# An encoder block with 64 streamed experts: the upper half of four late expert matrices loaded in transfers of eight partitions

## The chip, the core and the metric

The kernel runs on one core of a Trainium2 chip. The core has five engines that run their own instruction streams: TensorE (PE, matrix products; PEld is its weight load), VectorE (DVE), ScalarE (ACT), GpSimd (POOL) and SyncE (SP), which here does little but issue transfers. Sixteen DMA engines move the data between the chip's memory and the on-chip buffer, which has 128 partitions. The metric is the device time of one execution in microseconds, lower is better. Before the change it is 1477.58 us, the median of three runs (1474.58 to 1478.69).

## The reference, cut to what matters

One layer on 512 tokens of width 1024, in float32: a normalised projection, a convolution branch and an attention branch that are gated, merged and projected, and then a mixture of experts. There are 64 experts in 8 groups; every token takes the best group and in it the two best experts. Each expert has three matrices of 1024 x 512, 1024 x 512 and 512 x 1024, 2 MB each.

```
def mixer_block(u, ...):
    cb, cc, cx, q, k, v, gc, ga = split_columns(u @ w_in)
    y_conv = (cb * depthwise_conv_centred(cc * cx, conv_w)) @ w_conv_out
    y_attn = bidirectional_gqa(rope(rmsnorm(q)), rope(rmsnorm(k)), v) @ w_attn_out
    return (sigmoid(gc) * y_conv + sigmoid(ga) * y_attn) @ w_o

def hier_moe(u, w_group, w_router, w1, w3, w2):
    g = argmax(u @ w_group)                      # a group for each token
    top_v, top_i = top_k((u @ w_router)[g], 2)   # two experts in it
    def expert_block(xb, e):
        return (silu(xb @ w1[e]) * (xb @ w3[e])) @ w2[e]
    ...                                          # weighted sum of both experts

h = x + mixer_block(rmsnorm(x), ...)
out = h + hier_moe(rmsnorm(h), ...)
```

## The kernel before

The first 540 us or so are the mixer: projections of all 512 tokens with weights that SP loads in pieces of 512 KB and that ACT and DVE split in two parts. Behind it come the 64 experts, one after the other (the loop `for e in range(NE)`). For an expert, PE gathers up to 32 tokens with a selection matrix (`o_x`), multiplies them with w1 and w3 (`h`, 64 matrix products each; `hidden`), ACT and DVE form the gated product `gt`, and PE multiplies that with w2 (`y`, 32 products; `expert`). After every four experts PE scatters the results back to the tokens (`o_c`), and DVE adds them to `acc`. The last expert is written out apart (`last_expert`): its products are mixed with the scatter of the experts before it, and each finished piece of `acc` is stored at once.

The weights are numbered in the order of their use: matrix `i` belongs to expert `i // 3`, and `i % 3` says which of w1, w3 and w2 it is. `load_weight(i)` issues the load on SP's queue as one transfer of 128 partitions with 16 KB each (`nc.sync.dma_start`, line 601); the last matrix, 191, goes in two halves by columns. Nine buffers take turns, so the load of matrix `i` must wait until PE has read the matrix that was in the buffer. The loop issues the three loads of an expert ahead of that expert's work in the program, but SP runs ahead of PE as far as its waits allow.

A second wait is set by the framework and isn't in the kernel's text: a transfer that SP issues signals its end on one of eight semaphores, DMAHW0 to DMAHW7, which are taken in turn, and it is issued only when the transfer before it on that semaphore has landed. So at most eight of SP's transfers are under way. SP issues in program order, and what stands behind a waiting transfer waits too.

In the profile's rows all of this kernel's expert matrices are called `w`, and their issues stand at line 601.

Of the kernel before, what the change touches and what calls it, by code (L numbers as in the profile page):

```python
# [19 lines left out]
P = 128  # L20
# [11 lines left out]
CAP = 32  # L32
LOADS = (0, 1, 2, 4, 5)
CUTS = (0, 512, 1024)
OVB = 128
C_CB, C_CC, C_CX, C_Q, C_K, C_V, C_GC, C_GA = 0, 1024, 2048, 3072, 4096, 4352, 4608, 5632

# [2 lines left out]
def block_kernel(ctx, tc, x, norm1_g, w_in, conv_w, q_norm_g, k_norm_g, w_conv_out,  # L40
                 w_attn_out, w_o, norm2_g, w_group, w_router, w1, w3, w2, rope, out):
    nc = tc.nc
# [10 lines left out]
    def slot(i, shape, dt, name):  # L53
        return big.tile(shape, dt, tag=f"s{i}", name=name)
# [524 lines left out]
    wtiles = {}  # L579

    def weight_tile(i):
        shape = [P, 4, D] if i % 3 == 2 else [P, NK, FE]
        nm = f"{names[i % 3]}_{i // 3}"
        if i == len(order):
            return pools["mp"].tile(shape, F32, tag="acc", name=nm)
        return slot(order[(i if i < len(order) else i - 1) % len(order)], shape, F32, nm)

    def weight_source(i, e):
        if i % 3 == 2:
            return w2[e].rearrange("(p c) d -> p c d", c=4)  # L590
        return (w1, w3)[i % 3][e].rearrange("(p j) f -> p j f", j=NK)

    def rows(tile):
        return [tile[:, k, :] for k in range(tile.shape[1])]

    def load_weight(i):
        src = weight_source(i, i // 3)
        tile = weight_tile(i)
        cuts = CUTS if i == 3 * NE - 1 else (0, src.shape[2])
        for c0, c1 in zip(cuts, cuts[1:]):  # L600
            nc.sync.dma_start(tile[:, :, c0:c1], src[:, :, c0:c1])
        wtiles[i] = rows(tile)

    def load_unit(i):
        unit(lambda: load_weight(i))
# [23 lines left out]
    while nload < 10:  # L629
        load_weight(nload)  # L630
        nload += 1
# [137 lines left out]
    def overflow_table():  # L769
# [10 lines left out]
        for i in range(4):  # L780
            V.tensor_scalar(cnt[:, 1:2] if i else nblk[:, 0:1], cnt[:, 0:1], float(CAP + OVB * i), None, op0=OP.is_gt)
            if i:
# [10 lines left out]
        V.tensor_tensor(ov_base, io128[:, :NE], tab2[:, NE:2 * NE], op=OP.subtract)  # L793
        V.tensor_scalar(ov_base, ov_base, float(OVB), float(CAP), op0=OP.mult, op1=OP.add)
        ov_tab = mp.tile([1, NE + 1], I32, name="ov_tab")
# [42 lines left out]
    def slots_of(posm, gq):  # L838
        p0 = mp.tile(shp, F32, tag="p0", name="p0")
        es = slice(4 * gq, 4 * gq + 4)  # L840
        for t in range(NT):
            V.tensor_tensor(p0[:, t], posm[:, t, es, None].to_broadcast(shp[:1] + shp[2:]),
                            io32[:, None, :].to_broadcast(shp[:1] + shp[2:]), op=OP.is_equal)
        return p0
# [126 lines left out]
    for e in range(NE):  # L971
        while nload < min(3 * e + 3, 3 * NE):
            load_weight(nload)
            nload += 1
# [6 lines left out]
        elif e % 4 == 3 and e < NE - 1:  # L981
            p0 = slots_of(posm, e // 4 + 1)
# [12 lines left out]
        if e == 0:  # L995
            posm, W = finish_routing()
            p0 = slots_of(posm, 0)
# [42 lines left out]
```

## Time and profile before

| | us |
|---|---|
| median of the runs (lowest to highest) | 1477.58 (1474.58 to 1478.69) |
| profiled execution, its own time | 1474.83 |
| its span on the core | 1473.0 |
| PE busy in the span | 1207.8 (82%) |
| DVE, ACT, POOL busy | 460.5, 345.8, 88.1 |
| data moved | 449.71 MB |

The span runs from the first to the last instruction; 1.8 us lie around it. The page's second section cuts the span into 40 equal slices of 36.8 us. The DMA line in it gives the busy share of the sixteen DMA engines in tenths, the line under it what they moved. The page's fourth section follows the work that ended last backwards and says by which engine or transfer each part of the span was held. A wait of SP's own queue (SPq) is listed with what ended it. A transfer's landing time is counted from its issue, and so includes the time that it stands in line behind earlier transfers.

### The profile page before, as it was taken

Reading aid. Unit: us, or ns where it says so; the run is one execution under the profiler, and the core shown is the slowest. Engines: PE = TensorE matmul, PEld = TensorE weight load, DVE = VectorE, ACT = ScalarE, POOL = GpSimd, SP = SyncE. Lnnn points to the kernel's source line nnn. Section 1 sums busy time; section 2 is a strip of 40 time slices with the busy share of each in tenths; the row PEclk is TensorE's granted clock in tenths of the full one; section 3 lists DMA queues with packets and bytes.
Section 4 is the critical chain, followed back from the end, with each engine's and each line's share of the span. In section 5 each row is a group of like instructions: output and inputs, shape, how many; then the busy total and the mean of one; then the engine's idle time right before and its main releaser. Section 6 shows DMA issues by size and latency. Waiting matters only on the chain.

```text
span 1473.0 us, 33338 instructions
## 1 busy us (share of the span) xinstructions
PE 1207.8 (82%) x15152; PEld 902.4 (61%) x15152; DVE 460.5 (31%) x927; ACT 345.8 (23%) x716; POOL 88.1 (6%) x128
## 2 busy tenths in 40 slices
PE   7999999999999988888677785876867868678656
PEld 6788888888887866655454553544545545455443
DVE  4466666622225243132122120220211212212103
ACT  4344444422233131111111111111111111111101
POOL 2200000000002001000000000000000000000000
PEclk9999999999999999999898998988989979888989
DMA  6222222333354769999999999999999999999993
GB/s 165 59 86 65 66 70 72 93 110 97 101 193 128 322 237 426 423 427 425 426 426 426 425 426 427 425 427 424 426 426 426 426 424 426 427 425 425 427 412 146
DMA packets 109583, 449.71 MB, mean 305 GB/s; under 512 B 12544, under 2 KB 81152, under 8 KB 84992
## 3 DMA queue, kind: packets, MB, share of 16 engines
q1 hardware_dynamic: 108400, 447.55, 75.2%
q8 instruction: 120, 1.97, 0.5%
q10 hardware_dynamic: 1040, 0.00, 0.0%
q14 instruction: 23, 0.19, 0.0%
HBM read 445.44 MB, written 2.10 MB: 304 GB/s over the span
## 4 chain that ended last, share of the span: by engine, by line
PE 60%; DMA 35%; issue 2%; ACT 1%; DVE 1%; POOL 0%; SPq 0%; ACTq 0%; POOLq 0%; DVEq 0%
DMA w<-in_w 34%; PE o_c L74 8%; PE h L74 7%; PE o_g L74 6%; PE o_x L74 6%; PE y L74 5%; PE o_cb L74 3%; PE o_cx L74 3%; PE o_yc L74 3%; PE o_o L74 3%; PE o_q L74 3%; PE o_cc L74 3%; PE o_ya L74 2%; PE s L74 2%; PE o_pv L74 1%
## 5 line engine op out<-in xcount | busy, mean ns | idle before, releaser
L74 PE MATMUL h<-w,X 128*32 128x128 f32 x8192 | 296.7, 300 | 128.1 <-DMA w<-in_w 111.9
L74 PEld LDWEIGHTS h<-w,X 128*32 128x32 f32 x8192 | 258.8, 121 | 174.7 <-issue 81.7
L74 PE MATMUL y<-w,gt 128*32 128x256 f32 (+1 forms) x2080 | 152.1, 430 | 89.0 <-DMA w<-in_w 69.2
L74 PEld LDWEIGHTS y<-w,gt 128*32 128x32 f32 x2080 | 83.3, 121 | 140.0 <-issue 113.1
L890 ACT COPY Y<-y 32x256 f32<-32x256 f32 x252 | 91.4, 363 | 229.7 <-PE y L74 227.3
L158 DVE TENSOR_TENSOR wl<-raw,wh 128x1024 fp32r<-128x1024 f32 x76 | 98.6, 1298 | 140.8 <-ACT wh L157 139.4
L74 PE MATMUL o_x<-xt,pR 128*32 128x256 f32 x2048 | 133.9, 382 | 8.2 <-issue 4.8
L74 PE MATMUL o_c<-Y,S 128*128 128x512 f32 x256 | 121.9, 629 | 12.3 <-ACT Y L890 11.8
L157 ACT CAST wh<-raw 128x1024 fp32r<-128x1024 f32 x76 | 80.6, 1060 | 203.0 <-PE o_g L74 67.1
L831 DVE TENSOR_TENSOR acc<-o_c,acc 128x512 f32<-128x512 f32 x120 | 83.0, 692 | 114.0 <-PE o_c L74 114.0
L717 DVE STREAM_TRANSPOSE X<-xs 128x256 f32<-128x256 f32 x64 | 28.5, 445 | 281.6 <-PE h L74 244.6
L74 PEld LDWEIGHTS o_x<-xt,pR 128*32 128x32 f32 x2048 | 81.4, 110 | 42.0 <-issue 8.5
L872 DVE TENSOR_TENSOR sp<-h,sg 128x128 f32<-128x128 f32 x64 | 23.3, 364 | 264.3 <-ACT sg L868 264.3
L868 ACT ACTIVATE sg<-h 128x128 f32<-128x128 f32 x64 | 17.7, 277 | 374.6 <-PE h L74 374.6
L74 PEld LDWEIGHTS o_c<-Y,S 128*128 128x128 f32 x256 | 49.6, 200 | 78.1 <-issue 48.7
L74 PE MATMUL o_g<-u,wh 128*128 128x512 f32 x256 | 80.5, 395 | 0.0
L854 POOL TENSOR_TENSOR pR<-p,rstd 128x512 f32<-128x512 f32 x15 | 15.6, 1039 | 711.5 <-PE o_x L74 651.6
L74 PEld LDWEIGHTS o_g<-u,wh 128*128 128x128 f32 x256 | 48.1, 188 | 11.2
L74 PE MATMUL o_g<-u,wl 128*128 128x512 f32 x128 | 50.5, 395 | 0.0
L74 PE MATMUL o_q<-u,wh 128*128 128x512 f32 x128 | 40.3, 396 | 0.0
L74 PE MATMUL o_cc<-u,wh 128*128 128x512 f32 x128 | 40.2, 395 | 0.0
L74 PE MATMUL o_cb<-u,wh 128*128 128x512 f32 x128 | 40.1, 395 | 0.0
(221 smaller groups left out, 1418.7 us busy)
## 6 DMA issues: line engine op xcount, KB each, us to landing
w<-in_w SPq DMA_DIRECT2D x191, 2048.0 KB, 39.1
raw<-in_w_in SPq DMA_DIRECT2D x52, 512.0 KB, 3.8
raw<-in_w_conv_out SPq DMA_DIRECT2D x8, 512.0 KB, 4.1
raw<-in_w_attn_out SPq DMA_DIRECT2D x8, 512.0 KB, 4.1
raw<-in_w_o SPq DMA_DIRECT2D x8, 512.0 KB, 5.8
xt<-in_x SPq DMA_DIRECT2D x4, 512.0 KB, 7.0
w<-in_w SPq DMA_DIRECT2D x2, 1024.0 KB, 36.2
out<-acc SPq DMA_DIRECT2D x8, 256.0 KB, 2.1
```

The costliest lines, as they stand in the source:

```text
L74: return TE.matmul(o, l, r, start=start, stop=stop)
L157: A.copy(h, r)
L158: V.tensor_tensor(l, r, h.bitcast(F32), op=OP.subtract)
L717: V.transpose(X.rearrange("p j s -> p (j s)"), xs.rearrange("p j i -> p (j i)"))
L831: V.tensor_tensor(acc_at(t, n), o, xt[:, t, nsl] if first else acc_at(t, n), op=OP.add)
L854: eng.tensor_tensor(pR, p0.rearrange("p t e s -> p t (e s)"), rstd2[:, :, None].to_broadcast([P, NT, P]), op=OP.mult)
L868: A.activation(sg, h[:, 0:P], AF.Silu)
L872: V.tensor_tensor(sp.rearrange("p (c i) -> p c i", c=4), h[:, P:2 * P].rearrange("p (i c) -> p c i", c=4), sg.rearrange("p (i c) -> p c i" ...
L890: A.copy(d, y[32 * q:32 * q + 32, 0:256])
```

## The change

Four matrices, 174, 175, 177 and 178, are no longer loaded in one transfer. They are w1 and w3 of experts 58 and 59. Each is loaded as one transfer of its lower 64 partitions and eight transfers of eight partitions each for the upper 64. Matrix 176 (w2 of expert 58) and all others are loaded as before.

```
@@ -32,6 +32,7 @@
 LOADS = (0, 1, 2, 4, 5)
 CUTS = (0, 512, 1024)
+EIGHTHS = (174, 175, 177, 178)
 OVB = 128
@@ -596,6 +597,12 @@
     def load_weight(i):
         src = weight_source(i, i // 3)
         tile = weight_tile(i)
+        if i in EIGHTHS:
+
+            for p0, p1 in [(0, 64)] + [(b, b + 8) for b in range(64, P, 8)]:
+                nc.sync.dma_start(tile[p0:p1], src[p0:p1])
+            wtiles[i] = rows(tile)
+            return
         cuts = CUTS if i == 3 * NE - 1 else (0, src.shape[2])
```

On SP's queue before the change, this is the place from the second matrix of expert 57 to the first of expert 59. A row names the buffer and, behind the arrow, the source (w1, w3 or w2), the shape, and the semaphores that the issue waits for (DMAHW: the earlier transfer on the same semaphore; PE: the buffer's last reader).

```order
L601 DMA w3_57_11456<-in_w3 128x4096 [waits DMAHW3_49,PE_49]
L601 DMA w2_57_11458<-in_w2 128x4096 [waits DMAHW4_49,PE_49]
L601 DMA w1_58_11574<-in_w1 128x4096 [waits DMAHW5_49,PE_49]
L601 DMA w3_58_11576<-in_w3 128x4096 [waits DMAHW6_49,PE_49]
L601 DMA w2_58_11578<-in_w2 128x4096 [waits DMAHW7_49,PE_49]
L601 DMA w1_59_11694<-in_w1 128x4096 [waits DMAHW0_49,PE_49]
```

Every transfer has its own semaphore here and is a whole matrix, so eight under way are eight matrices.

The same place on SP's queue after the change, from the first matrix of expert 58 to the lower half of the second:

```order
L608 DMA w2_57_11458<-in_w2 128x4096 [waits DMAHW4_49,PE_49]
L603 DMA w1_58_11574<-in_w1 64x4096 [waits DMAHW5_49,PE_49]
L603 DMA w1_58_11574<-in_w1 8x4096 [waits DMAHW6_49]
L603 DMA w1_58_11574<-in_w1 8x4096 [waits DMAHW7_49]
L603 DMA w1_58_11574<-in_w1 8x4096 [waits DMAHW0_49]
L603 DMA w1_58_11574<-in_w1 8x4096 [waits DMAHW1_49]
L603 DMA w1_58_11574<-in_w1 8x4096 [waits DMAHW2_49]
L603 DMA w1_58_11574<-in_w1 8x4096 [waits DMAHW3_49]
L603 DMA w1_58_11574<-in_w1 8x4096 [waits DMAHW4_49]
L603 DMA w1_58_11574<-in_w1 8x4096 [waits DMAHW5_49]
L603 DMA w3_58_11584<-in_w3 64x4096 [waits DMAHW6_49,PE_49]
```

The matrix takes nine semaphores where it took one. The seven issues from DMAHW6 to DMAHW4 wait for the seven whole matrices before it, the last one of which is w2 of expert 57; the eighth one (DMAHW5) waits for the lower half of its own matrix.

## Rows read from the trace of the kernel before

**Rows 1.** The page: the chain that ended last, shares by engine and line.

```profile
PE 60%; DMA 35%; issue 2%; ACT 1%; DVE 1%; POOL 0%; SPq 0%; ACTq 0%; POOLq 0%; DVEq 0%
DMA w<-in_w 34%; PE o_c L74 8%; PE h L74 7%; PE o_g L74 6%; PE o_x L74 6%; PE y L74 5%; PE o_cb L74 3%; PE o_cx L74 3%; PE o_yc L74 3%; PE o_o L74 3%; PE o_q L74 3%; PE o_cc L74 3%; PE o_ya L74 2%; PE s L74 2%; PE o_pv L74 1%
```

**Rows 2.** The same chain in order of time, near the end: start, length, what.

```profile
1366.88 36.93 DMA w<-in_w
...
1403.87 39.57 DMA w<-in_w
1443.44 0.14 issue
1443.58 1.81 PE h L74 x32
...
1461.06 5.36 PE o_c L74 x12
```

**Rows 3.** Stretches of the span: busy time by engine, granted clock, DMA share, GB/s.

```profile
core 0: us, PE busy (x) PEld busy (x) DVE busy (x) ACT busy (x) POOL busy (x), PEclk, DMA share, GB/s
1200.00:1280.00 80.00, 57.36 (x977) 39.43 (x970) 13.65 (x32) 12.16 (x34) 2.51 (x5) 0.84 1.01 426
...
1430.00:1434.00 4.00, 1.13 (x34) 0.83 (x24) 0.00 (x0) 0.00 (x0) 0.00 (x0) 0.94 0.99 390
1434.00:1438.00 4.00, 3.14 (x52) 2.34 (x46) 0.47 (x2) 0.28 (x1) 0.00 (x0) 0.63 0.61 253
1438.00:1442.00 4.00, 1.93 (x32) 1.13 (x32) 0.22 (x1) 1.45 (x4) 0.00 (x0) 1.00 0.50 205
1442.00:1446.00 4.00, 2.42 (x33) 1.89 (x34) 0.00 (x0) 0.00 (x0) 0.00 (x0) 0.72 0.50 213
1446.00:1450.00 4.00, 4.00 (x38) 1.83 (x37) 1.38 (x2) 0.00 (x0) 0.00 (x0) 0.85 0.49 183
1450.00:1454.00 4.00, 4.00 (x41) 1.69 (x39) 2.07 (x3) 0.00 (x0) 0.00 (x0) 1.00 0.28 108
```

**Rows 4.** DMA queues (packets, MB, share of 16 engines' span) and issues (KB, us).

```profile
q1 hardware_dynamic: 108400, 447.55, 75.2%
q8 instruction: 120, 1.97, 0.5%
...
w<-in_w SPq DMA_DIRECT2D x191, 2048.0 KB, 39.1
...
out<-acc SPq DMA_DIRECT2D x8, 256.0 KB, 2.1
...
wr<-in_w_group SPq DMA_DIRECT2D x1, 32.0 KB, 3.0
...
g2j<-in_norm_g SPq DMA_DIRECT2D x1, 4.0 KB, 2.4
```

**Rows 5.** Waits of SP's queue from 1200 us on: total us, times, longest.

```profile
SPq L601 <- DMA w<-in_w: 162.0, 43, 4.9
...
SPq L601 <- PE h L74: 29.4, 11, 5.0
SPq L601 <- PE y L74: 11.2, 4, 3.0
```

**Rows 6.** The tile w: SP's issues, min/median/max ns, and the landing times.

```profile
L601 SPq DMA_DIRECT2D w<-in_w x193: 327/328/6116, 291.0 to 1418.5; - x193
...
DMA to landing us min/median/max: 7.9/39.1/40.8
```

**Rows 7.** PE near the end, in order of time: idle before, and what ended it.

```profile
1389.16 3.59 PE L74 MATMUL h<-w,X 128*32 128x128 f32 x64 [2.85 <-DMA w<-in_w]
```

More of the change, by code (lines that the diff above doesn't have):

```diff
@@ L34 @@
 CUTS = (0, 512, 1024)
+EIGHTHS = (174, 175, 177, 178)
 OVB = 128
@@ L598, in load_weight @@
         tile = weight_tile(i)
+        if i in EIGHTHS:
+            for p0, p1 in [(0, 64)] + [(b, b + 8) for b in range(64, P, 8)]:
+                nc.sync.dma_start(tile[p0:p1], src[p0:p1])
+            wtiles[i] = rows(tile)
+            return
         cuts = CUTS if i == 3 * NE - 1 else (0, src.shape[2])
```

## The prediction

> **What bounds the kernel now.** I read the shares of the chain that ended last first [rows 1]: after PE, the loads of the expert matrices are the largest part of it, 34% of the span. Its end in order of time [rows 2] then shows where: from 1366.88 us to 1443.44 us it is almost nothing but these loads. After the last wait for a load, PE, ACT and DVE need 1473.0 - 1443.44 = 29.6 us to the end, and the change touches nothing there. The stretches [rows 3] show why the loads bind: in the steady part the DMA share is 1.01 and the engines move 426 GB/s, while PE is busy for 57.36 of 80 us. A matrix of 2048.0 KB [rows 4], 2,097,152 bytes, thus takes 4.92 us, one engine brings 426 / 16 = 26.6 GB/s, and PE uses 72% of that time. PE waits before a set of products for the load, not the other way round [rows 7]. So what delays or hastens the last loads moves the end by as much.
>
> Two more things are to be seen. First, SP's issues wait mainly for earlier transfers: 162.0 us against 40.6 us for PE [rows 5]. A matrix lands 39.1 us after its issue [rows 6], which is eight times 4.92 us: eight transfers are under way, and all eight count, whatever their size. Second, the sixteen engines don't end together [rows 3]: the share falls from 0.99 at 1430 to 1434 us to 0.50 from 1438 to 1446 us, at 205 to 213 GB/s, although the last matrix had been issued by 1418.5 us [rows 6]. I read this as eight engines that are done near 1434.5 us and eight that work until about 1452 us: a lag of some 18 us (0.61 over 1434 to 1438 us is a full share for 0.9 us and half of it after; 0.28 from 1450 us on is half for 2.2 us). A cause of that size is there: the instruction queue took 0.5% of 16 engines' span [rows 4], 0.005 x 16 x 1473 = 118 us of engine time, or 14.7 us on each of eight engines. Let me call them the early and the late half.
>
> **The change part by part.** *Issues.* Four transfers become 36, so 32 more issues at 0.327 us [rows 6], 10.5 us of SP in all. Nine for a matrix take 2.9 us, less than the transfer of one; SP has nothing else to do there, so I cost them at nothing. Without that cover it would be up to 10.5 us.
>
> *Bytes.* The same, but they may go to other engines. An eighth is 128 KB in eight rows. I assume eight engines with one row each, all eight times the same ones; if these are the early half, the early half gets 64 KB more and the late half 64 KB less for each engine and matrix: four times 2.46 us either way, 9.84 us.
>
> *The new wait.* The lower half of matrix 174 and the first seven eighths are issued when the eight whole matrices before it land, one every 4.92 us. In these 39.4 us the early half gets only the lower half (2.46 us) and seven eighths. It has 39.1 - 18 = 21 us of older work in line, and then runs dry: its lead is not passed on to the late half but lost as idle time. The eighth one waits for the lower half of 174, which the late half moves 2.46 us after matrix 173, and matrix 175 stands behind it on SP. From issue to first data I take 1.5 us (a store of 256.0 KB lands after 2.1 us [rows 4], of which 0.6 us is the transfer at 426 GB/s). So both halves are empty about 4.0 us after 173 has landed, and only then goes on. From there eight transfers under way are hardly one matrix.
>
> *The price of an eighth.* The trace before has no such transfer. From below: eight engines at 26.6 GB/s each, 0.62 us. From above: in the steady part sixteen engines fill 128 partitions, eight partitions get 26.6 GB/s, and nothing shows that they can take more; then it's 131,072 B / 26.6 GB/s = 4.92 us. In between stands that a group of four neighbouring partitions shares one way in: two engines' rates, 2.46 us. I take 2.46 us. The nearest rows are those of the small transfers, whatever holds them: they landed after 2.1 us for 256 KB, 2.4 us for 4 KB and 3.0 us for 32 KB [rows 4], none sooner.
>
> [...]
>
> *The sum,* from the landing of matrix 173 to that of 191, 18 matrices, 88.6 us before. After: 4.0 us until the flow starts again; 25 eighths (the last of 174, and those of 175, 177, 178) at 2.46 us, 61.5 us; three lower halves at 2.46 us, 7.4 us; 14 whole matrices at 4.92 us, 68.9 us. That is 141.8 us, or +53.2 us. The first seven eighths of 174 hide in the wait, but if ways in are shared, they take their time from the late half, which fills the upper partitions at 213 GB/s: 7 x 131,072 B / 213 GB/s = 4.3 us. The late half's instruction packets no longer count in the last 90 us: 1% of them, -1 us. So +56.5 us: 1474.83 + 56.5 = 1531.3 us for the profiled execution. That one lies 2.75 us under the median of its kernel; the median comes to 1534 us. PE follows: its products for a matrix, at most 3.6 us even at a low clock [rows 7], fit in 4.92 us.
>
> **The rivals.**
>
> *The engines are the limit, not the way in.* An eighth costs 0.62 us, so 25 of them 15.4 us: 4.0 + 15.4 + 7.4 + 68.9 = 95.7 us, +7.1, less 1: +6 us, 1484 us. For it: sixteen engines at 26.6 GB/s is all the rows show, and a limit elsewhere need not exist. Against it: eight engines have never been seen writing to eight partitions. If the late half gets the eighths, nothing of them hides: 4 x 2.46 = 9.8 us, 1487 us. Which half it is no row tells. [...]
>
> *The two halves are evened out* (the other side). The early half ends 9.84 us later, near 1444.3 us, the late one 9.84 us earlier, near 1442.4 us: the loads end 7.9 us before 1452.2 us, and the time is 1470 us. For it: the lag of 18 us is real, and twice 9.84 us is just its size. It decides on the early half having its additional work in line before it runs dry: that needs some 16 transfers under way at 174, and eight are let through. It also needs eighths at 0.62 us.
>
> *All eight partitions share one way in:* 4.92 us an eighth, 25 of them 123 us: 4.0 + 123 + 7.4 + 68.9 = 203.3 us, +114.7 and +3.3 as above, 1596 us. Against it: a way so narrow would have no reserve over the one engine that uses it before.
>
> *The change doesn't do what it says:* an eighth is spread over all sixteen engines. Then no lag is moved, but the waits stay: the same sum with 0.31 us for an eighth, 4.0 + 7.7 + 7.4 + 68.9 = 88.0 us, no change, 1477 us. Eight rows would have to be cut for it.
>
> **How the numbers follow.** Forecast 1534 us, chance 0.58, by itself 1515 to 1560 (the refill of 4.0 us and the sharing of 4.3 us each up to twice, or the eighths partly apart in time). The engine limit, 1481 to 1488 us, 0.23. Evened out, 1470 us, 0.08. One way in, 0.05. No change, 0.03. The rest, 0.03, lies between 1488 and 1515 us. The range from 1480 to 1560 us leaves out the gain, most of no change and the one way, about 0.16. A measurement of this kernel can tell about 0.3%, 4.4 us, from no change. Faster 0.08; same 0.05, with the low edge of the engine limit; slower 0.87.
>
> **What the profile after would show.** SP's waits for `w` at the new line 603, 4.92 us each for the first seven, then about 2.5 us each (0.6 us if the engines are the limit). The landing time of an eighth in the rest near 8 x 2.46 = 20 us. A DMA share near one third to one half, and some 110 GB/s or less, for about 80 us from 1365 us on, then 426 GB/s again. PE waiting some 20 us each for w1 and w3 of expert 58 and 59. The end of the loads without the step at half share, or a shorter one. I would be wrong in kind if the loads ended earlier, and in the price if the stretch at low rate were 25 us long.

## The result and the profile after

The changed kernel takes 1543.86 us, the median of four runs (1528.98 to 1551.09), against 1476.16 us before: a ratio of 1.0437, 95% interval 1.0394 to 1.0480, or +67.7 us. The forecast was 1534 us with a range of 1480 to 1560 us. The profiled execution took 1538.8 us with a span of 1537.0 us, 64.0 us more than before.

First the packets, from the page of the kernel before and then of the changed one.

```profile
DMA packets 109583, 449.71 MB, mean 305 GB/s; under 512 B 12544, under 2 KB 81152, under 8 KB 84992
```

```profile
DMA packets 109839, 449.71 MB, mean 293 GB/s; under 512 B 12800, under 2 KB 81408, under 8 KB 85248
```

The bytes are the same, and there are 256 more packets, all under 512 B. They stand against 32 more transfers, so each adds eight. The two experiments with halves below add four transfers of 64 partitions and 64 packets (12608), 16 for each. I read the small packet as the end of one engine's part in a transfer: an eighth is then the work of eight engines, a half that of sixteen.

Stretches of the changed kernel, with the columns of [rows 3]:

```profile
1340.00:1350.00 10.00, 9.16 (x23) 3.75 (x16) 4.33 (x7) 1.45 (x4) 0.00 (x0) 0.72 1.05 382
1350.00:1360.00 10.00, 7.43 (x182) 5.58 (x184) 2.07 (x5) 1.24 (x3) 0.00 (x0) 1.00 0.80 188
...
1370.00:1380.00 10.00, 7.67 (x182) 5.51 (x178) 1.26 (x4) 0.65 (x2) 0.00 (x0) 1.00 0.47 120
...
1390.00:1400.00 10.00, 0.00 (x0) 0.00 (x0) 0.00 (x0) 0.00 (x0) 0.00 (x0) 0.50 0.97 126
1400.00:1405.00 5.00, 0.00 (x0) 0.00 (x0) 0.00 (x0) 0.00 (x0) 0.00 (x0) 0.50 0.81 157
1405.00:1415.00 10.00, 3.64 (x64) 3.22 (x64) 1.26 (x4) 0.65 (x2) 0.00 (x0) 0.50 0.89 156
1415.00:1425.00 10.00, 3.64 (x32) 1.57 (x32) 0.00 (x0) 1.45 (x4) 0.00 (x0) 0.50 0.63 118
...
1456.00:1490.00 34.00, 19.58 (x356) 13.08 (x356) 4.36 (x12) 4.25 (x14) 0.00 (x0) 0.85 1.01 427
```

Two shorter stretches, inside these:

```profile
1415.30:1419.20 3.90, 3.64 (x32) 1.57 (x32) 0.00 (x0) 0.12 (x1) 0.00 (x0) 0.50 0.49 101
1432.60:1436.20 3.60, 3.55 (x64) 3.22 (x64) 0.00 (x0) 0.00 (x0) 0.00 (x0) 0.50 0.55 114
```

For about 100 us from 1350 us on, the engines move 118 to 188 GB/s where they moved 426; then the old rate is back. The row of 1390 to 1400 us is the one to look at: the DMA share is 0.97 and the rate 126 GB/s. The engines are not out of work, they are held up inside their packets: by the trace's packet records, a packet of 16 KB takes 0.61 us in the steady part, and the 41 that begin between 1395 and 1400 us take 2.1 to 2.2 us each. So the share of 0.97 says here that an engine has a packet open, not that bytes flow at the old rate. Between 1370 and 1380 us, with a share of 0.47, half of them are out of work as well. In the two shorter stretches only about eight engines work (shares of 0.49 and 0.55), on the lower half of matrix 177 and of 178, and they move 101 and 114 GB/s; eight engines alone moved 205 to 213 GB/s in the kernel before [rows 3].

PE in the same place, the first products of matrices 174 to 178, with the wait before each:

```profile
1384.48 1.96 PE L75 MATMUL h<-w,X 128*32 128x128 f32 x64 [2.63 <-DMA w<-in_w]
1405.21 3.64 PE L75 MATMUL h<-w,X 128*32 128x128 f32 x64 [18.77 <-DMA w<-in_w]
1415.38 3.64 PE L75 MATMUL y<-w,gt 128*32 128x256 f32 x32 [6.53 <-DMA w<-in_w]
1432.65 3.64 PE L75 MATMUL h<-w,X 128*32 128x128 f32 x64 [13.63 <-DMA w<-in_w]
1451.53 3.52 PE L75 MATMUL h<-w,X 128*32 128x128 f32 x64 [15.23 <-DMA w<-in_w]
```

Waits of 14 to 19 us stand before w3 of expert 58 and w1 and w3 of expert 59, where [rows 7] had 2.85 us. The products take 3.64 us instead of 1.96 us: the granted clock is 1.00 from 1384 to 1390 us and 0.50 from 1390 to 1450 us, where PE has no product until 1405.21 us. That costs nothing: the next load isn't there.

SP's issues of the eighths (start, length), each row from a short window of its own. An issue that waits for the transfer eight places before it tells when that one landed: the last rise of matrix 169's semaphore is at 1346.67 us, the issue that waits for it at 1346.69 us.

```profile
1341.80 0.27 SPq L603 DMA_DIRECT2D w<-in_w  x1
1346.69 0.27 SPq L603 DMA_DIRECT2D w<-in_w  x1
1354.94 0.27 SPq L603 DMA_DIRECT2D w<-in_w  x1
1363.28 0.27 SPq L603 DMA_DIRECT2D w<-in_w  x1
1369.12 0.27 SPq L603 DMA_DIRECT2D w<-in_w  x1
1375.94 0.27 SPq L603 DMA_DIRECT2D w<-in_w  x1
1379.80 0.27 SPq L603 DMA_DIRECT2D w<-in_w  x1
...
1384.15 0.27 SPq L603 DMA_DIRECT2D w<-in_w  x1
1389.61 0.27 SPq L603 DMA_DIRECT2D w<-in_w  x1
...
1404.99 0.27 SPq L603 DMA_DIRECT2D w<-in_w  x1
1415.26 0.27 SPq L603 DMA_DIRECT2D w<-in_w  x1
1420.51 0.27 SPq L603 DMA_DIRECT2D w<-in_w  x1
...
1432.58 0.27 SPq L603 DMA_DIRECT2D w<-in_w  x1
1437.59 0.27 SPq L603 DMA_DIRECT2D w<-in_w  x1
...
1451.50 0.33 SPq L608 DMA_DIRECT2D w<-in_w  x1
```

The first six rows are the second to the seventh eighth of matrix 174 and mark the landing of the whole matrices 168 to 173. The distance is 4.89 us once, then 8.25, 8.34, 5.84 and 6.82 us: the late engines lose time as soon as the early ones write the parts of 174. The other rows mark, in turn, the landing of

- 174: the lower half (1379.80) and the last eighth (1384.15);
- 175: the lower half (1389.61) and the last eighth (1404.99);
- 176, loaded whole (1415.26);
- 177: the lower half (1420.51) and the last eighth (1432.58);
- 178: the lower half (1437.59) and the last eighth (1451.50).

So a lower half took 5.46, 5.25 and 5.01 us; the eight eighths of a matrix took 15.38, 12.07 and 13.91 us, 1.5 to 1.9 us for one and 1.72 us on average; and the whole matrix 176 took 10.27 us, twice the 4.92 us of the steady part.

### The profile page after: what moved, and what is told of

Read it like the earlier page. It is cut to its first block, busy times and chain, and to the rows that moved or that the text cites. A ratio compares the mean times of both kernels' runs of the same rounds, so it can differ in the third digit from the quotient of the medians.

```text
span 1537.0 us, 33384 instructions
## 1 busy us (share of the span) xinstructions
PE 1224.7 (80%) x15152; PEld 909.6 (59%) x15152; DVE 461.4 (30%) x927; ACT 346.2 (23%) x716; POOL 88.8 (6%) x128
## 4 chain that ended last, share of the span: by engine, by line
PE 52%; DMA 43%; issue 2%; DVE 1%; ACT 1%; another core or an unknown queue 0%; POOL 0%; SPq 0%; ACTq 0%; POOLq 0%; DVEq 0%
DMA w<-in_w 42%; PE h L75 6%; PE o_g L75 6%; PE o_c L75 6%; PE y L75 4%; PE o_x L75 4%; PE o_q L75 3%; PE o_cb L75 3%; PE o_cx L75 3%; PE o_yc L75 3%; PE o_o L75 3%; PE o_cc L75 3%; PE o_ya L75 2%; PE s L75 1%; PE o_pv L75 1%
## 5 line engine op out<-in xcount | busy, mean ns | idle before, releaser
L75 PE MATMUL h<-w,X 128*32 128x128 f32 x8192 | 299.9, 302 | 166.3 <-DMA w<-in_w 144.6
L75 PEld LDWEIGHTS h<-w,X 128*32 128x32 f32 x8192 | 262.0, 122 | 215.1 <-issue 118.0
L75 PE MATMUL y<-w,gt 128*32 128x256 f32 (+1 forms) x2080 | 158.7, 445 | 95.9 <-DMA w<-in_w 74.3
```

The source lines that it names most:

```text
L75: return TE.matmul(o, l, r, start=start, stop=stop)
```

## The experiments

Three theories were held against each other. A: neighbouring partitions share one way in, with about the rate of one engine. B: what costs is the number of transfers, since only eight may be under way. D came up later: two transfers of 1 MB for a matrix are dear by themselves. Each kernel below was timed beside the kernel before. All but one change the list of slices that `load_weight` runs over for the four matrices; the one changes which matrices are cut. Where a landing is given from semaphore events, it is read from the trace itself, which lists every rise of a semaphore. The kernel before has 4736 for its 296 transfers, sixteen for each; in the changed kernel an eighth has nine, one 0.44 to 0.83 us after its issue and eight later. I read each of the sixteen, and of the eight, as the end of one engine's part.

**Eighths with a step of four partitions.**

```
-  [(0, 64)] + [(b, b + 8) for b in range(64, P, 8)]
+  [slice(0, 64)] + [slice(h + b, h + b + 29, 4) for h in (64, 96) for b in range(4)]
```

> The same 36 transfers of the same sizes in the same order, with the same waits; only which eight partitions an eighth fills is changed: every fourth one (64, 68, ..., 92, then 65, ..., and so on) instead of eight neighbours. Theory A (neighbouring partitions share one way in, so four engines that write to four neighbours share the rate of one): each of the eight engines now has a group of four to itself, an eighth costs 0.62 us instead of about 2, and 25 of them are 30 to 46 us cheaper; what stays is the refill and what the late engines lose, so +10 to +25 us against the kernel before. Theory B (what costs is the number of transfers and that only eight may be under way): nothing changes, +60 to +70 us.

1509.42 us against 1477.67: ratio 1.0206 (1.0181 to 1.0231), +31.8 us. With the same transfers, bytes and waits, 36 of the 67.7 us are gone. By the semaphore events the eighths of matrix 175 land 0.62 us apart here (1387.67, 1388.29, 1388.91, 1389.53 us), where eighths of neighbours took 1.5 to 1.9 us. B falls as the whole cause. But A's 10 to 25 us were too low: something else costs.

**Eighths with a step of eight, and of two.**

```
+  e2_step8: [slice(0, 64)] + [slice(64 + b, P, 8) for b in range(8)]
+  e7_step2: [slice(0, 64)] + [slice(h + b, h + b + 15, 2) for h in (64, 80, 96, 112) for b in range(2)]
```

> As the changed kernel, but an eighth fills every eighth partition from 64 to 127 (64, 72, ..., 120). Theory A with groups of four neighbours alone: no two engines of an eighth share a group, so it costs what the step of four costs, +10 to +25 us. Theory A with the addition that the group 32 partitions further on shares the same way in: two engines on each way, an eighth of 1.2 us, 25 times 0.6 us more than the step of four: between the two, +25 to +42 us. Theory B: +60 to +70 us.

> As the changed kernel, but an eighth fills every second partition of sixteen neighbours (64, 66, ..., 78, then 65, ..., 79, then 80, ...): two engines in each group of four neighbours, four groups. Theory A: the price of an eighth goes with the number of engines at one way in, and this is as dear as the step of eight, where two engines meet through the groups 32 partitions apart: +40 to +53 us. If the step of eight is dear for another reason than the groups 32 apart: anything else between the step of four (+32 us) and the eight neighbours (+68 us).

Step of eight: 1524.52 us, ratio 1.0312 (1.0290 to 1.0333), +46.9 us. Step of two: 1518.12 against 1476.90 us, ratio 1.0284 (1.0264 to 1.0304), +41.2 us. The intervals overlap, and both stand between the step of four and the neighbours. In the step of eight no two partitions are neighbours, and yet it's dearer than the step of four. What its partitions have in common is a distance of 32: I conclude that groups of four that lie 32 apart share one way in too. So 1, 2 and 4 engines at one way give +32, +41 to +47 and +68 us. That a group has four partitions is my assumption; it fits these runs, which do not measure it by itself.

The 2.46 us for an eighth of neighbours, which the prediction took from two engines' rates, were too high: it was 1.72 us on average. Whether a way takes more than the rate of one engine, or the eight engines were not all at the same eighth, no run tells.

**Eight pieces by columns.**

```
+  for k in range(NK):
+      nc.sync.dma_start(tile[:, k, :], src[:, k, :])
```

> The same four matrices in eight transfers each, but cut by columns: every transfer has all 128 partitions with 2 KB each, 256 KB. So 32 transfers instead of 4, eight under way are one matrix, and all sixteen engines and all partitions take part in each. Theory A: no way in is shared, the late engines stay supplied; 0 to +6 us (shorter packets, the early engines' lead lost). Theory B: the line runs as empty as in the changed kernel: +45 to +65 us.

1479.19 us, ratio 1.0014 (1.0002 to 1.0026), +1.5 us. Thirty-two transfers instead of four cost next to nothing when each takes in all partitions. The stretch where they are issued:

```profile
1360.00:1370.00 10.00, 8.51 (x212) 6.68 (x208) 1.01 (x4) 1.02 (x3) 0.00 (x0) 1.00 0.60 230
1370.00:1380.00 10.00, 7.83 (x192) 5.10 (x191) 0.24 (x2) 1.46 (x4) 0.00 (x0) 1.00 1.01 368
```

At a share of 0.60 the early half has run dry here too, as the prediction said of the eight slots. As no work was moved to it, that costs nothing: the late half sets the end.

**Only the first of the four matrices.**

```
-EIGHTHS = (174, 175, 177, 178)
+EIGHTHS = (174,)
```

> Of the four matrices only 174 is loaded in a lower half and eight eighths of neighbours. It holds apart what is paid once and what is paid by the matrix. Theory A: matrix 174's first seven eighths are issued while older loads are under way; the price is what the late engines lose to them, about 9 us in the changed kernel's trace, and one eighth and the refill, some 4 us: +8 to +15 us, less than a quarter of the whole. Theory B: a quarter, +15 to +18 us, if every matrix costs the same.

1491.83 us, ratio 1.0095 (1.0067 to 1.0123), +14.2 us. It lies in A's range, and near B's quarter as well, so it doesn't tell them apart (B has fallen by the step of four). It bounds the price of the first matrix, most of whose eighths were supposed to hide.

**Two halves, lower and upper.**

```
+  [slice(0, 64), slice(64, P)]
```

> Each of the four matrices in two transfers, partitions 0 to 63 and 64 to 127; all sixteen engines take part in both, so no work moves between the early and the late engines, and eight transfers under way are still four matrices. It tells what the lower half alone costs. Theory A, with 64 partitions holding only eight ways in: a half may take 4.9 us and not 2.46 us wherever early and late engines are at the same half at the same time; between 0 and four times 4.9 us, +3 to +20 us. If a half is not shared in that way: 0 to +3 us.

1516.04 us, ratio 1.0270 (1.0253 to 1.0287), +39.1 us: more than either guess, with no eighth in it and only four transfers more. Stretches of this kernel:

```profile
1340.00:1350.00 10.00, 9.57 (x96) 5.21 (x97) 5.54 (x8) 1.68 (x5) 0.00 (x0) 1.00 1.03 387
1350.00:1360.00 10.00, 8.72 (x180) 6.02 (x174) 2.45 (x6) 2.48 (x7) 0.00 (x0) 1.00 1.00 223
1360.00:1370.00 10.00, 5.64 (x128) 4.13 (x127) 0.00 (x0) 0.74 (x2) 0.00 (x0) 1.00 1.02 219
1370.00:1380.00 10.00, 7.66 (x131) 4.54 (x131) 1.26 (x4) 0.65 (x2) 0.00 (x0) 0.83 1.00 257
...
1430.00:1440.00 10.00, 7.66 (x139) 5.30 (x134) 2.68 (x6) 2.10 (x6) 0.00 (x0) 0.90 0.99 423
```

All sixteen engines are busy, at half the rate; by theory A, because 64 partitions of one half have only half of the ways. On average that makes 39.1 / 8 = 4.9 us for each of the eight halves. But 16.3 us of it are lost before the first half has landed: SP's issues put the landing of the whole matrices 169 to 173 at 1345.82 and 1381.74 us, 35.9 us for four matrices that take 19.6 us at the steady rate. So the late engines, still at whole matrices, run at little more than half their speed too while the early ones are at the halves. Why, these runs don't tell.

**Two halves, even and odd partitions.**

```
+  [slice(0, P, 2), slice(1, P, 2)]
```

> Each of the four matrices in two transfers of 64 partitions, the even-numbered and the odd-numbered ones, in place of the lower and the upper half (that cost 39 us). Number, size and waits of the transfers are the same as with the halves. Theory A: each engine then has four of eight neighbouring partitions, two groups of four, and all sixteen ways in are in use at any time: 0 to +5 us. Theory D (two transfers of 1 MB per matrix cost this, whichever partitions they fill): +39 us.

1477.20 us against 1477.42: ratio 0.9999 (0.9988 to 1.0011). Nothing is left of the 39 us, with the same number and size of transfers. D falls. The same place:

```profile
1350.00:1360.00 10.00, 10.00 (x219) 7.44 (x214) 2.44 (x6) 2.86 (x8) 0.00 (x0) 1.00 1.01 426
1360.00:1370.00 10.00, 8.99 (x223) 6.83 (x219) 1.26 (x4) 1.02 (x3) 0.00 (x0) 1.00 0.99 404
```

**Lower and upper half exchanged.**

```
+  [slice(64, P)] + [slice(h + b, h + b + 29, 4) for h in (0, 32) for b in range(4)]
```

> The kernel with the step of four turned round: partitions 64 to 127 in one transfer first, then eight transfers of every fourth partition in the lower half. It tells which partitions the late engines fill. If they are the upper ones (the early engines then write the eighths of matrix 174 where nobody else writes while the late ones are still at work): cheaper than the step of four in the upper half, +15 to +27 us. If the late engines fill the lower half: as dear or dearer, +32 to +40 us.

1500.99 us, ratio 1.0157 (1.0134 to 1.0180), +24.1 us, 8 us less than with the same steps in the upper half; the intervals just don't meet (1.0180, 1.0181). I take it that the late engines fill the upper partitions, and that eighths there are in their way. The traces bear this out only in part. From the landing of matrix 169 to that of 173, while the late engines are at whole matrices, this kernel takes 25.7 us (issues at 1347.95 and 1373.69 us) and the one with steps in the upper half 27.1 us (1347.52 and 1374.65 us); most of the 8 us come later. So which half fills which partitions is argued, not shown.

**Nine transfers, none of which crowds a way.**

```
+  [slice(0, P, 2)] + [slice(h + b, h + b + 29, 4) for h in (0, 32, 64, 96) for b in (1, 3)]
```

> Nine transfers for each of the four matrices as in the changed kernel: the 64 even-numbered partitions first, then eight eighths of odd-numbered ones, each with a step of four, so that neither the first transfer nor an eighth crowds a way in. Theory A with the lower half as a cost of its own: what is left is the refill and the early engines' additional bytes, +7 us by the sum of the prediction with 0.62 us for an eighth, and up to 5 us for what the late engines lose: +6 to +14 us. If the lower half costs nothing of its own: as the step of four in the upper half, +32 us.

1489.61 us, ratio 1.0079 (1.0062 to 1.0096), +12.2 us. In its trace, first while the eighths are issued and then at the end of the loads:

```profile
1350.00:1360.00 10.00, 10.00 (x216) 7.87 (x214) 2.45 (x6) 2.85 (x8) 0.00 (x0) 1.00 0.61 240
1360.00:1370.00 10.00, 8.84 (x218) 6.63 (x212) 1.26 (x4) 1.02 (x3) 0.00 (x0) 1.00 0.51 174
1390.00:1400.00 10.00, 2.84 (x56) 2.33 (x52) 0.00 (x0) 1.45 (x4) 0.00 (x0) 0.69 0.66 239
...
1456.00:1460.00 4.00, 3.08 (x32) 1.40 (x27) 0.00 (x0) 0.83 (x3) 0.00 (x0) 0.68 0.98 418
1460.00:1464.00 4.00, 3.29 (x50) 1.89 (x54) 0.95 (x2) 0.62 (x2) 0.00 (x0) 1.00 0.98 390
1464.00:1468.00 4.00, 3.40 (x60) 1.90 (x54) 1.82 (x3) 0.00 (x0) 0.00 (x0) 1.00 0.82 302
```

The step at half share that stood at the end of the loads before [rows 3] is nearly gone: by the semaphore events of the last load the two halves end 5 us apart (1467.29 and 1472.27 us), where it was 16.7 us before (1436.88 and 1453.60 us). Even so the kernel is slower. Here share and rate fall together, unlike in the changed kernel: the engines are out of work, not held up. That is the price of the eight slots, and it is more than the evening-out gives back.

No run beat the kernel before.

## Why the prediction was right

**The total.** The runs part the +67.7 us in three. What stays when no way is crowded (work moved to engines that run dry): 12.2 us. The lower halves as blocks: 31.8 - 12.2 = 19.6 us, 4.9 us for each of the four. The eighths as neighbours: 67.7 - 31.8 = 35.9 us. The first difference also holds what upper eighths cost more than odd ones all over. All are medians, and the total itself is known to some 6 us either way. The measured 1543.86 us also lies in the narrower 1515 to 1560 us that the prediction gave to this mechanism by itself.

**The issues** were rightly costed at nothing: an eighth's issue takes 0.27 us, nine for a matrix about 2.6 us, and the eight column pieces cost 1.5 us in all.

**The new wait** was right in place and kind. The first seven eighths waited for the seven matrices before, the early half ran dry (a share of 0.47), and the eighth one was issued when the lower half of 174 had landed. One thing was wrong in it: I took all eight engines of an eighth for early ones. By the semaphore events six are early and two late. Of the first eighth of 174, six parts had landed by 1359.2 us and two only at 1375.4 and 1376.2 us, together with matrix 173; every kernel with eighths shows the same six and two. So the first seven eighths didn't land while the older matrices did, but at 1376.15 to 1382.93 us.

**What the late half loses** before matrix 173 has landed was mis-sized: 9.6 us (1375.94 us, where four times 4.9 us after 1346.69 would be 1366.3), not 4.3 us. I had counted only the bytes of the eighths, and no run shows that the late half fills the upper partitions, as the 4.3 us have it. The single matrix in eighths, +14.2 us, bears the size out. The eighths of neighbours are the smaller part of it: the same stretch loses 7.5 us with the step of four, 16.3 us with two halves and no eighth, and 1.1 us with nine transfers that crowd no way (issues at 1344.41 and 1365.12 us).

**The rest of the sum,** from the landing of 173 to that of 178's last eighth, against the rows of SP's issues:

| us | sum | trace |
|---|---|---|
| until the lower half of 174 has landed | 4.0 | 3.9 |
| the last eighth of 174 | 2.5 | 4.3 |
| three lower halves | 7.4 | 15.7 |
| 24 eighths | 59.0 | 41.4 |
| the whole matrix 176 | 4.9 | 10.3 |
| together | 77.8 | 75.6 |

**The price of an eighth** was chosen too high: 2.46 us, against 1.72 us. In us this is the largest error, 17.6 us. The choice between 0.62 and 4.92 us was the right one, and the step of four shows why. That four neighbours share one way in was assumed there; no row of the kernel before shows it, and the runs showed +32 us with one engine to a group of four, +41 us with two and +68 us with four.

**The lower halves** were wrong by a factor of two: 2.46 us each, as if they had no way to share. They took 5.0 to 5.5 us, and the two halves tell it by themselves. If four neighbours and the four 32 further on share one way, as the step of eight suggests, 64 partitions have eight ways and not sixteen; by my estimate a lower half then takes 4.92 us, which makes the sum 7.4 us higher.

**The whole matrix 176** stands between cut ones and was taken at its steady price. By the semaphore events eight engines had finished it by 1406.43 us and gone on to the lower half of 177, while the eight that write eighths finished it only at 1414.18 to 1415.25 us; in that stretch the engines move 156 GB/s at a share of 0.89.

That the sum came within 2.2 us over this stretch is luck: an eighth too dear makes up for lower halves and a matrix 176 too cheap. Against five matrices at 4.92 us the 75.6 us are +51 us, with the 9.6 us +60.6 us of 64.0. Most of the remaining 3.4 us stands ahead of the change and may be the spread between executions: matrix 169 landed at 1346.67 us here and at 1343.52 us in the profiled execution of the kernel before. The mechanism (neighbours crowd each other, SP's eight places hold the rest back) was not luck; the experiments bear it out.

**The rivals.** That the engines alone are the limit (+6 us) falls with the steps: the price goes with the crowding, though the engines' work is the same. It describes the uncrowded version best, which needed twice as much, 12.2 us. The evening-out does occur there, at the end of the loads, but the point I named decides: eight slots don't keep the early half supplied. One way in for eight partitions would have been 4.92 us an eighth; none was seen. An eighth over all sixteen engines is excluded by the eight packets.

Three of the signs named for the profile were off. The share was not near one third to one half throughout but up to 1.05, since engines that are held up count as busy. I gave the low stretch 80 us; it was about 100 us, because it begins with the late half's loss. And of the four long waits of PE the one for w1 of expert 58 didn't come (2.63 us). The lag between the halves was a little smaller than the 18 us that I read: 16.7 us by the semaphore events of the last load before the change.

**Why the uncrowded version needs 12 us and not 6** is largely the two late engines of each eighth: there, too, the first seven eighths of 174 land only behind matrix 173 (1365.10 us), and the last one lands at 1374.67 us, 9.6 us after it, where the sum had 4.0 + 0.62 us.

**Open.** Why a half of 64 partitions costs about 4.9 us more, where 2.5 us would do if sixteen engines shared eight ways evenly for that time alone, is explained in part. The eight engines that came last to the lower halves of 177 and 178 had them to themselves and still ran at half speed (101 and 114 GB/s), so eight engines crowd each other as sixteen do; two of them at each way would explain it, but no row tells which partitions an engine takes. Why the late engines slow down while they are at whole matrices stays open. And all edits that choose other partitions also choose other rows of the source in the chip's memory, since a partition's 16 KB are one run there. That the crowding is at the ways into the partitions, and not where the rows are read, is argued from the pattern (four neighbours, and those 32 apart); no run parts the two.

## What to carry to other kernels

Read the DMA share and the rate together: here a share of 1.00 to 1.02 at 219 to 223 GB/s, half of 426, was crowding, and a share of 0.51 at 174 GB/s a lack of work. A load that goes in parts of the partitions is better spread over the whole range than cut in blocks: every second partition over all 128 cost nothing here (ratio 0.9999), two blocks of 64 cost 39.1 us. And before a load is cut up to move work between DMA engines, count how many transfers may be under way, eight on SP's queue here: pieces use up the slots that keep the faster engines supplied, and with no way crowded that still cost 12.2 us.

## What the runs showed of the hardware that I had not expected

- Loading by halves costs 39 us for four matrices when the halves are blocks of 64 partitions, and nothing (ratio 0.9999, 0.9988 to 1.0011) when they are the even and odd ones.
- Half of the DMA engines lag by some 17 us at the end of the kernel before. Six of the eight engines that write an eighth belong to the other half, and two to the one that lags (of the first eighth, six parts landed by 1359.2 us, two at 1375.4 and 1376.2 us). That the instruction packets cause the lag is argued from their sum alone.
- Eight engines that load 64 neighbouring partitions alone run at half speed (101 GB/s, where eight alone moved 205 to 213 GB/s before), and engines at whole matrices slow down while others are at such a block (16.3 us in the kernel with two halves).
- The runs of the changed kernel spread over 22 us (1528.98 to 1551.09), those of the kernel before over 4 us, and those of the even and odd halves over 6 us. The other crowded kernels spread over 3 to 6 us, so crowding alone doesn't explain it.
